# A 32-byte tile at the head of a pool of a Trainium2 kernel (GLA, HGRN2, mLSTM and a convolutional FFN, one step)

## The chip, the cores and the metric

The kernel runs on one core of one Trainium2 chip. The metric is the device time of one execution in microseconds. The program is one launch; its five engines are TensorE (PE; its weight loads are listed as PEld), VectorE (DVE), ScalarE (ACT), GpSimd (POOL) and SyncE (SP, which only issues transfers here).

## The reference

One inference step of a one-layer encoder over 1024 prompt frames and 32 frames of a running stream, all float32. A mixer of three kinds of recurrent heads is followed by a feed-forward part with a causal convolution; the change touches the last matrix product.

```python
def conv_ffn(xn, buf, w_up, conv_w, conv_b, w_down):
    up = xn @ w_up                                      # (T, 1024) @ (1024, 5632)
    up, buf = causal_dwconv(up, buf, conv_w, conv_b)
    gate, val = jnp.split(up, 2, axis=-1)
    return (jax.nn.gelu(gate, approximate=True) * val) @ w_down, buf    # (T, 2816) @ (2816, 1024)
...
h, st_new = mixer(rms_norm(x, g_mix_pre[l]), st, lb_all[l], w_in[l], ...)
x = x + rms_norm(h, g_mix_post[l])
h, ffn_buf = conv_ffn(rms_norm(x, g_ffn_pre[l]), ...)
x = x + rms_norm(h, g_ffn_post[l])
```

## The kernel before

The program runs in this order: input projection and mixers (interleaved), output projection (`zp`, with the weight `woh`/`wol` as moving operand and the transposed rows `ch`/`cl` as stationary one), up projection (accumulators `pux`, `puw`, `puy`, `puz`), down projection (accumulators `q`, `x`), final norm.

Every large product is made of three matmuls. A float32 operand is split into a rounded half and the rest (`split`, lines 105 to 110: ScalarE copies the rounded half, line 107, and VectorE subtracts for the rest, line 110). `mm3` (lines 100 to 103) then adds half x half (L101), half x rest (L102) and rest x half (L103) into one accumulator; its first operand is stationary, its second moving. In the profile such a matmul reads `out<-moving,stationary`.

The up and the down projection use a seven-product (Strassen) form. For the down projection, `down_all` runs seven kinds of product in the order P2, P1, P4, P6, P5, P7, P3. Each kind has 11 blocks (`NP`), one per pair of feature tiles. A block has two operands of 512 columns: `h` from rows of the activated hidden layer (`hts`, loaded by `load_h`) and `w` from the weight (`wraws`, loaded by `down_raw`, or its sums prepared in DRAM, `ws_d`). `down_operands` splits both. `run` then makes, for each of four 128-column slices of `h` as stationary operand, an `mm3` with all 512 columns of `w` moving into one of four accumulator banks: 12 matmuls of 128x512 a block, 132 a kind, 924 in all. During P2 and P1, `sample_products` (line 1462) adds four narrower float32 matmuls a pair of blocks for the 32 stream frames, straight from `ht` and the raw weight. During P4 and P6 VectorE also makes the sums of hidden rows that later kinds need (lines 1497 to 1506). After each of the four row slices of P3, VectorE, ScalarE and GpSimd norm the rows and SyncE stores them (lines 1635 to 1637).

The kernel is written in a framework that orders each engine's instructions by its own model of time, and that places tiles in SBUF pool by pool, each tile on a multiple of 32 bytes in its partition. The places follow from the code, and the built program lists them. The pool `ph` is opened by `freed` (line 1754), which runs in the last block of the up projection, when the pool `px` of the up projection's operands has been closed. It holds the hidden rows `ht11` to `ht21`, four raw weight buffers, four `h` operands (tag `hop`), and one early `w` operand, that of P2's first block, which `ahead` splits with `early=True`. All other `w` operands lie in the pool `p4` (`praw[1]`, tag `op`), two raw weight buffers in `p4r`. A row of 1060 float32 is 4240 bytes and takes up 4256 in the pool; all other tiles of `ph` have 4096.

Byte addresses in the partition, as built, before the change:

| operand | tiles | first address | modulo 64 | modulo 512 |
|---|---|---|---|---|
| `h` of the down projection (stationary) | 4 in `ph`, 4096 apart | 83,680 | 32 | 224 |
| `w` of the down projection (moving) | 7 in `p4`, 4096 apart | 25,856 | 0 | 256 |
| `w` of P2's first block | in `ph` | 95,968 | 32 | 224 |
| raw weights in `ph` | 4 | 63,040 | 0 | 64 |
| `ht11`, `ht12`, ... | in `ph` | 54,528 | 0 and 32 | varies |
| `woh`, `wol` of `zp` (moving) | in `p2` | 147,360; 180,128 | 32 | 416 |
| `ch`, `cl` of `zp` (stationary) | in `p2`, 2048 apart | 216,992; 223,136 | 32 | 416 |
| up projection, stationary | in `p4` | 25,856 | 0 | 256 |
| up projection, moving, 272 columns | in `px` | 54,528 | 0 | in steps of 64 |
| up projection, moving, 256 columns | in `px1` | 156,640 | 32 | 480 |

The rest of a split operand lies 2048 bytes behind its rounded half, and a slice of 128 columns 512 bytes behind the one before it.

Of the kernel before, what the change touches and what calls it, by code (L numbers as in the profile page):

```python
# [8 lines left out]
F32 = mybir.dt.float32  # L9
# [82 lines left out]
def body(ctx: ExitStack, tc: tile.TileContext, a: dict):  # L92
# [1236 lines left out]
    def up_finish(py, f, uu):  # L1329
# [15 lines left out]
        sp.dma_start(h_d[f], ys[0])  # L1345

    def up_all(pw_, W0, X, uus, py, freed, ahead, begun):

        raw, W, summed = {}, {0: W0}, []
        late = None  # L1350
        for f in range(NF):
            uu = uus[f % len(uus)]
            if f + 1 < NF:
                raw[f + 1] = up_raw(f + 1)
            for s in range(2):
                if s == 1 and f + 1 < NF:
                    ops = up_operands(f + 1, raw.pop(f + 1))
                    W[f + 1] = next(ops)
                    for _ in ops:
                        pass  # L1360
                if f or s:
                    blk = up_block(pw_, f, s, W[f], X[s], uu)
                    next(blk)
                    next(late, None)
                    if f == NF - 1 and s == 1:
                        freed()
                    m = (2 * f + s - 3) * len(SUMS) // 34
                    while len(summed) < min(m, len(SUMS)):
                        sum_weights(*SUMS[len(summed)])
                        summed.append(m)  # L1370
                    if s == 0:
                        up_finish(py(), f - 1, uus[(f - 1) % len(uus)])
                        W.pop(f - 1)
                    next(blk)
                else:
                    blk = begun
                yield
                next(blk)
                late = blk
                yield  # L1380
# [4 lines left out]
    praw, ph, EARLY = [], [], 3  # L1385
# [24 lines left out]
    def down_raw(kind, p):  # L1410

        key = (kind, p if kind in ("P1", "P2") else p // 2)
        if key in wraws:
            return
        own = len(wraws) % 6 < 2
        r = (praw[0] if own else ph[0]).tile([128, 2, 512], F32, tag="raw", name=f"wr{kind}_{p}", bufs=2 if own else 4)
        if kind in ("P1", "P2"):
            f = p + NP * (kind == "P2")
            behind["SP"] = sp.dma_start(r.rearrange("p j n -> p (j n)"), a["w_dn"][f])
        else:  # L1420
            n = min(2, NP - p)
            src = a["w_dn"][NP + p:NP + p + n, :, 512:].rearrange("f p n -> p f n") if kind == "P3" else \
                ws_d[{"P5": 0, "P7": 1, "P6": 2, "P4": 3}[kind]][:, p:p + n, :]
            behind["SP"] = sp.dma_start(r[:, :n, :], src)
        wraws[key] = r
# [3 lines left out]
    def load_h(pool_, f):  # L1429
        hts[f] = pool_.tile([128, NCOL], F32, name=f"ht{f}")  # L1430
        with tc.issue_after(behind["SP"].ins):
            sp.dma_start(hts[f], h_d[f])
# [321 lines left out]
    def freed():  # L1754
        pxs.close()
        ph.append(phs.enter_context(tc.tile_pool(name="ph", bufs=1, side="left")))
        for p in range(EARLY):
            down_raw("P2", p)
            load_h(ph[0], NP + p)
        down_raw("P2", EARLY)  # L1760
# [5 lines left out]
    for i, _ in enumerate(up_all(pw_, W0, X, uus, lambda: py[0], freed, ahead, blk)):  # L1766
        if i == 1:

            with tc.issue_after(done[0].ins), tc.issue_after(kept["c6"].ins):
                for x in last:  # L1770
                    next(x)
            X[1] = col_operands([px1] * 2, {f"B{k + 1}{j + 1}": x1[:, 4 * k:4 * k + 4, j, :] for k in range(2) for j in range(2)}, 1)
            p6s.close()
            p5s.close()
            py.append(p9s.enter_context(tc.tile_pool(name="p9", bufs=1, side="right")))
# [140 lines left out]
```

## Time and profile before

| | us |
|---|---|
| median of 3 runs | 1386.83 |
| lowest, highest | 1385.41, 1388.37 |
| the profiled execution | 1389.22 |
| its span, first to last instruction | 1387.5 |
| its mean granted TensorE clock | 0.983 of full speed |

The down projection's matmuls start at 1143.8 us of the span and the last one starts at 1377.1 us; what follows is the norm and the store of the last rows. In the profile's list of instructions in order of time each row has a start, a duration, the engine, the line, the operation with `out<-in`, the shapes and a count. Neighbouring rows of equal kind are merged, with the count behind `x`. The duration of a matmul contains a modelled end and overlaps with its successor, so the time that a matmul takes of the engine is the step from its start to the next one's. In the table of stages, a row has the stretch, its length, then each engine's busy time with its number of instructions, the granted TensorE clock (1.00 is full speed), and the DMA share and rate.

### The profile page before, as it was taken

The numbers are of one execution on the slowest core, as the hardware profiler recorded it, in microseconds if no ns is written. First come the engines' busy times: TensorE is split into PE (matmuls) and PEld (weight loads), VectorE is DVE, ScalarE is ACT, GpSimd is POOL, SyncE is SP. The second block draws the span as 40 slices with busy tenths as digits, with TensorE's granted clock in tenths as the row PEclk, the third lists the DMA queues.
The fourth block names the chain that finished last, engine by engine and source line by source line (L and its number), as shares of the span: only waits on it lengthen the run. The fifth ranks groups of instructions, "written<-read, shape, count | busy, mean of one in ns | idle before, by whom it ended". The sixth has DMA issues, their size and how long they took to land.

```text
span 1387.5 us, 29219 instructions
## 1 busy us (share of the span) xinstructions
PE 1341.0 (97%) x11472; PEld 1206.8 (87%) x11472; DVE 1029.7 (74%) x1916; ACT 706.6 (51%) x1369; POOL 316.0 (23%) x529
## 2 busy tenths in 40 slices
PE   6999999999999999999989999999999999999997
PEld 5999889898889887867889999999999996678885
DVE  4786568768587569685888888888888876498556
ACT  4555547446474446342665545545555544444552
POOL 5532411225112154222111112121121110010005
PEclk9999999999999998999999999999999999999999
DMA  8599869776789936443413475555365239645425
GB/s 342 199 326 350 276 228 307 235 263 228 249 263 322 310 96 211 152 142 90 165 52 135 142 176 146 142 142 160 108 169 135 89 133 392 245 155 152 129 99 122
DMA packets 125825, 269.72 MB, mean 194 GB/s; under 512 B 24007, under 2 KB 59367, under 8 KB 125607
## 3 DMA queue, kind: packets, MB, share of 16 engines
q1 hardware_dynamic: 111959, 245.43, 52.4%
q0 software_dynamic: 8928, 18.09, 7.0%
q10 hardware_dynamic: 4800, 4.33, 0.9%
q8 instruction: 90, 1.47, 0.4%
q14 instruction: 48, 0.39, 0.1%
HBM read 206.72 MB, written 86.18 MB: 211 GB/s over the span
## 4 chain that ended last, share of the span: by engine, by line
PE 76%; DVE 10%; ACT 5%; DMA 4%; issue 2%; POOL 1%; SPq 1%; DVEq 0%; POOLq 0%; ACTq 0%
PE pux L101 5%; PE pux L102 5%; PE pux L103 4%; PE pv L101 4%; PE pv L103 4%; PE pv L102 3%; PE puw L102 3%; PE puw L103 3%; PE puw L101 3%; PE q L101 3%; PE q L102 3%; PE q L103 3%; PE x L101 2%; PE x L102 2%; PE x L103 2%
## 5 line engine op out<-in xcount | busy, mean ns | idle before, releaser
L1341 DVE SCALAR_TENSOR_TENSOR y<-uu,fconv_sb,y 128x1060 f32<-128x1060 f32 x88 | 116.3, 1321 | 35.5 <-ACT y L1339 34.6
L1277 ACT COPY c<-pux 128x272 f32<-128x272 f32 (+1 forms) x132 | 49.4, 377 | 52.1 <-PE pux L103 48.5
L101 PE MATMUL pv<-wt_0h,xh 128*128 128x256 f32 (+2 forms) x195 | 57.9, 297 | 6.7 <-ACT xh L321 4.8
L1339 ACT ACTIVATE y<-uu,fconv_sb 128x1060 f32<-128x1060 f32 x44 | 56.3, 1279 | 11.8 <-POOL uu L1335 10.4
L101 PE MATMUL zp<-woh,ch 128*128 128x512 f32 (+1 forms) x144 | 60.0, 418 | 1.9 <-DVE z L1156 1.2
L1338 POOL COPY fhalo<-uu 128x2 f32<-128x2 f32 x44 | 16.6, 376 | 188.0 <-DVE uu L1282 188.0
L102 PE MATMUL zp<-wol,ch 128*128 128x512 f32 (+1 forms) x144 | 58.3, 405 | 0.0
L103 PE MATMUL zp<-woh,cl 128*128 128x512 f32 (+1 forms) x144 | 58.3, 406 | 0.0
L103 PE MATMUL pv<-wt_0h,xl 128*128 128x256 f32 (+2 forms) x195 | 56.9, 292 | 0.4 <-DVE xl L322 0.4
L102 PE MATMUL pv<-wt_0l,xh 128*128 128x256 f32 (+2 forms) x195 | 56.4, 289 | 0.1
L103 PE MATMUL pv<-wt_1h,xl 128*128 128x256 f32 (+2 forms) x195 | 56.5, 290 | 0.0
L102 PE MATMUL pv<-wt_1l,xh 128*128 128x256 f32 (+2 forms) x195 | 56.2, 288 | 0.0
L101 PE MATMUL pv<-wt_1h,xh 128*128 128x256 f32 (+2 forms) x195 | 56.1, 288 | 0.0
L1517 POOL TENSOR_TENSOR gss<-gss 128x1 f32<-128x1 f32 (+1 forms) x9 | 7.8, 868 | 191.0 <-ACT gjk L1510 191.0
L220 POOL TENSOR_SCALAR hrs<-hss 128x5 f32<-128x5 f32 (+3 forms) x27 | 9.9, 367 | 161.5 <-DVE hss L922 160.0
L431 POOL TENSOR_TENSOR vg<-vth,gh 128x256 f32<-128x256 f32 (+1 forms) x36 | 30.6, 851 | 63.6 <-DMA vm<-v_d 23.3
L101 PEld LDWEIGHTS pv<-wt_0h,xh 128*128 128x128 f32 (+1 forms) x195 | 37.1, 190 | 8.9 <-ACT xh L321 5.7
L851 DVE TENSOR_TENSOR Qz<-x,qe 128x128 f32<-128x128 f32 (+1 forms) x106 | 29.9, 300 | 12.3 <-PE sc L720 11.7
L815 DVE COPY_PREDICATED P<-masks_sb,sc 128x352 f32<-128x352 int32 (+1 forms) x44 | 29.8, 677 | 12.4 <-PE sc L720 12.2
L103 PEld LDWEIGHTS pv<-wt_0h,xl 128*128 128x128 f32 (+1 forms) x195 | 37.2, 191 | 1.2 <-DVE xl L322 0.9
L102 PEld LDWEIGHTS pv<-wt_0l,xh 128*128 128x128 f32 (+1 forms) x195 | 37.2, 191 | 0.6 <-POOL wt_0l L110 0.5
L101 PEld LDWEIGHTS pv<-wt_1h,xh 128*128 128x128 f32 (+1 forms) x195 | 37.1, 190 | 0.4 <-issue 0.2
(1718 smaller groups left out, 5409.4 us busy)
## 6 DMA issues: line engine op xcount, KB each, us to landing
wrP<-in_w_dn SPq DMA_DIRECT2D x27, 512.0 KB, 3.7
h_d<-y SPq DMA_DIRECT2D x22, 530.0 KB, 2.8
ht<-h_d SPq DMA_DIRECT2D x22, 530.0 KB, 8.8
wt_0r<-in_w_tok SPq DMA_DIRECT2D x21, 512.0 KB, 5.6
wt_1r<-in_w_tok SPq DMA_DIRECT2D x21, 512.0 KB, 6.7
ws_d<-in_w_dn POOLq DMA_DIRECT2D x20, 512.0 KB, 9.3
wrP<-ws_d SPq DMA_DIRECT2D x20, 512.0 KB, 4.0
wt_0l<-lt_d SPq DMA_DIRECT2D x14, 512.0 KB, 3.9
```

Source lines behind the costliest of these rows:

```text
L101: pe.matmul(ps, lh[0], rh[0], start=first, stop=False, **kw)
L102: pe.matmul(ps, lh[0], rh[1], start=False, stop=False, **kw)
L103: return pe.matmul(ps, lh[1], rh[0], start=False, stop=last, **kw)
L220: pool.tensor_scalar(out, ss, 1.0 / width, eps, op0=ALU.mult, op1=ALU.add)
L431: pool.tensor_tensor(o[:n], th[:n], gh[:n, c0:c0 + 256], op=ALU.mult)
L815: dve.copy_predicated(dst, mk.broadcast_to([n, 11, *mk.shape[2:]]), src)
L851: dve.tensor_tensor(Qp[:, 2 * i, :, :n // 2].rearrange("p e (m c) -> p e m c", c=c), second(x4[:, f:f + 1], c).broadcast_to([128, 2, n // ...
L1277: kept[name] = act.copy(t, ps)
L1338: behind["POOL"] = pool.tensor_copy(fhalo[:, j, :], u[:, NCOL - 2:NCOL])
L1339: act.activation(y, u, AF.Identity, scale=fconv[:, j, 2:3], bias=fconv[:, j, 3:4])
L1341: dve.scalar_tensor_tensor(y, uu[i][:, s:s + NCOL], fconv[:, j, s:s + 1], y, op0=ALU.mult, op1=ALU.add)
L1517: pool.tensor_tensor(ss[:n, 0:1], ss[:n, 2:3], ss[:n, 3:4], op=ALU.add)
```

## The change

`freed` allocates one more tile, of 8 float32 a partition, as the first one in `ph`. No instruction reads or writes it.

```diff
     def freed():
         pxs.close()
         ph.append(phs.enter_context(tc.tile_pool(name="ph", bufs=1, side="left")))
+        ph[0].tile([128, 8], F32, name="pad")
         for p in range(EARLY):
             down_raw("P2", p)
             load_h(ph[0], NP + p)
```

All 123 tiles that are placed in `ph` lie 32 bytes higher: `h` at 83,712 and so on (0 modulo 64, 256 modulo 512), the early `w` at 96,000 (0 and 256), the raw weights in `ph` at 63,072 (32 modulo 64); the rows `ht` swap, those at 0 modulo 64 going to 32 and those at 32 to 0. No other tile moves. The instructions of each engine, their order and their waits are the same as before.

## The prediction

> **What bounds the kernel now.** I read the page first, then the stages of the down projection, then the times at which single matmuls start.
>
> ```profile
> PE 1341.0 (97%) x11472; PEld 1206.8 (87%) x11472; DVE 1029.7 (74%) x1916; ACT 706.6 (51%) x1369; POOL 316.0 (23%) x529
> PE 76%; DVE 10%; ACT 5%; DMA 4%; issue 2%; POOL 1%; SPq 1%; DVEq 0%; POOLq 0%; ACTq 0%
> ```
>
> TensorE works through 97% of the span and carries 76% of the chain that ended last. The change touches only the down projection, the last 240 us. Its stages, with the busy time of each engine:
>
> ```profile
> core 0: us, PE busy (x) PEld busy (x) DVE busy (x) ACT busy (x) POOL busy (x), PEclk, DMA share, GB/s
> 1143.00:1183.00 40.00, 40.00 (x197) 28.25 (x197) 22.82 (x34) 18.32 (x31) 0.56 (x3) 1.00 1.01 395
> 1183.00:1223.00 40.00, 38.20 (x177) 24.11 (x175) 22.06 (x35) 17.98 (x33) 0.00 (x0) 1.00 0.63 234
> 1223.00:1253.00 30.00, 30.00 (x130) 23.96 (x129) 28.98 (x49) 14.23 (x31) 4.82 (x3) 1.00 0.40 121
> 1253.00:1285.00 32.00, 32.00 (x139) 25.71 (x138) 27.67 (x46) 16.64 (x31) 1.64 (x2) 1.00 0.48 144
> 1316.00:1346.00 30.00, 30.00 (x130) 24.12 (x129) 15.71 (x26) 13.68 (x26) 0.00 (x0) 1.00 0.38 132
> ```
>
> PE has no idle time but 1.8 us where P2 hands over to P1, and its granted clock is 1.00. So the stage ends when TensorE has streamed its matmuls, and what counts is the step from one start to the next. Here are the first starts of P7 and its last one:
>
> ```profile
> 1315.72 0.39 PE L101 MATMUL x<-P7w,P7h 128*128 128x512 f32 x1
> 1315.95 0.40 PE L102 MATMUL x<-P7w,P7h 128*128 128x512 f32 x1
> 1316.19 0.39 PE L103 MATMUL x<-P7w,P7h 128*128 128x512 f32 x1
> ...
> 1346.29 0.40 PE L103 MATMUL x<-P7w,P7h 128*128 128x512 f32 x1
> ```
>
> P7 has 11 blocks of 12 matmuls, 132; from its first to its last start are 131 steps, 30.57 us, **233.4 ns** a step. (The 0.39 us beside each is a modelled end; neighbours overlap.)
>
> The kernel has another phase of the same shape, three-term products of 512 moving columns on a 128x128 stationary: the output projection, `zp`. Its last unit, then unit 6:
>
> ```profile
> 672.21 0.39 PE L102 MATMUL zp<-wol,ch 128*128 128x512 f32 x1
> ...
> 681.05 0.39 PE L102 MATMUL zp<-wol,ch 128*128 128x512 f32 x1
> 658.64 0.39 PE L103 MATMUL zp<-woh,cl 128*128 128x512 f32 x1
> ...
> 660.90 0.39 PE L101 MATMUL zp<-woh,ch 128*128 128x512 f32 x1
> 671.00:681.00 10.00, 10.00 (x45) 8.26 (x45) 9.01 (x10) 8.48 (x21) 1.14 (x3) 1.00 0.59 211
> ```
>
> 39 steps in 8.84 us are **226.7 ns**, at the same clock 1.00, though VectorE and ScalarE are busier around it (9.01 and 8.48 of 10 us) than around P7 (15.71 and 13.68 of 30). Unit 6 changes the accumulator bank after every third matmul, as the down projection does, and still takes 2.26 us for 10 steps. So neither the clock, nor other engines, nor the change of banks makes the 6.7 ns between the two phases. What is left is where the operands lie. In `zp` the moving operand (`woh`, `wol`) and the stationary one (`ch`, `cl`) have the same remainder, 416, modulo 512 bytes, and every slice that a matmul takes keeps it. In the down projection the moving `w` has remainder 256 and the stationary `h` 224: 32 bytes apart.
>
> **The change part by part.** No instruction is added, removed or moved, and no wait; 123 tiles of `ph` lie 32 bytes higher. Four things can follow.
>
> *Products.* `h` gets remainder 256 modulo 512, as `w` has: the two operands are then placed to each other as in `zp`. Of the 924 products the first block of P2 already had equal remainders (its `w` is allocated in `ph` too and moves along), so 912 change. At zp's step that is 912 x (233.4 - 226.7) ns = 6.1 us. Whether this comes from the equal remainders is not shown by two phases alone, and the one block inside P2 with equal remainders reads:
>
> ```profile
> 1144.47 0.39 PE L102 MATMUL q<-P2w,P2h 128*128 128x512 f32 x1
> 1144.69 0.39 PE L103 MATMUL q<-P2w,P2h 128*128 128x512 f32 x1
> 1144.92 0.40 PE L102 MATMUL q<-P2w,P2h 128*128 128x512 f32 x1
> ...
> 1146.79 0.39 PE L101 MATMUL q<-P2w,P2h 128*128 128x512 f32 x1
> ```
>
> 10 steps in 2.32 us, 232 ns, with one step of 0.22 that P7 doesn't show: neither phase's rhythm. But zp also needs some matmuls after a break to find its own:
>
> ```profile
> 616.59 0.40 PE L102 MATMUL zp<-wol,ch 128*128 128x512 f32 x1
> ...
> 618.45 0.39 PE L101 MATMUL zp<-woh,ch 128*128 128x512 f32 x1
> ```
>
> These first 8 steps after a transpose take 1.86 us, 232 ns, like the block of P2. The bounds of the price are therefore 233.4 ns (no gain) and 226.7 ns (6.1 us); I take the second, less what breaks cost.
>
> *Breaks.* The sample rows' matmuls interrupt the products:
>
> ```profile
> L1462 PE MATMUL s<-wrP,ht x88: 592/605/618, 1153.0 to 1222.7; 128*32 128x512 f32 x88
> 1191.08 1.07 PE L1462 MATMUL s<-wrP,ht 128*32 128x512 f32 x8
> ```
>
> Eight a group make 11 groups; with the start of P2 and two pauses at the handover to P1, 14 breaks. Each loses up to 8 x (232.5 - 226.7) = 46 ns of the gain: 0.6 us. The sample matmuls' own operands move as well (`ht`, and four of six weight buffers from a multiple of 64 to 32 past one). Nothing shows their price; scaled by the same 6.7/233.4 to either side, the 88, some 1.07 us a group, could move by 11 x 1.07 x 2.9% = 0.3 us. I take 0 and keep both ends.
>
> *VectorE, ScalarE and transfers.* The split of `h` writes, and that of `w` reads, at shifted addresses:
>
> ```profile
> L110 DVE TENSOR_TENSOR P2h<-ht,P2h x11: 685/690/693, 1142.6 to 1175.9; 128x512 fp32r<-128x512 f32 x11
> L110 DVE TENSOR_TENSOR P2w<-wrP,P2w x11: 684/689/694, 1136.0 to 1170.0; 128x512 fp32r<-128x512 f32 x11
> ```
>
> One writes 32 past a multiple of 64, the other on one, and both take 684 to 694 ns: price 0. VectorE could still eat the gain where it is nearly full, 28.98 of 30 us in P4. The tightest operand there, `h` of block 4, is ready at 1235.22 and first needed at 1236.39:
>
> ```profile
> 1234.55 0.67 DVE L110 TENSOR_TENSOR P4h<-ht,P4h 128x512 fp32r<-128x512 f32 x1
> 1236.39 1.10 PE L103 MATMUL q<-P4w,P4h 128*128 128x512 f32 x4
> ```
>
> VectorE's burst begins with sums that wait for the end of P1, so it starts earlier by what P2 and P1 save; the 4 blocks of P4 before this use save 48 x 6.7 = 0.3 us, under the 1.17 us of slack. That cover holds. In P2, whose first 40 us run at DMA share 1.01, a faster TensorE asks for its loads sooner; if loads set its pace, its 132 products lose at most 0.9 us, which I put into the range.
>
> *The end.* The last 48 matmuls finish the four row blocks one after another, each followed by a chain on VectorE:
>
> ```profile
> 1369.12 0.69 DVE L1635 TENSOR_TENSOR ca<-ca,q 128x512 f32<-128x512 f32 x1 [1.45 <-PE q L103]
> 1379.32 0.69 DVE L1635 TENSOR_TENSOR ca<-ca,q 128x512 f32<-128x512 f32 x1
> ```
>
> The first waits for PE, the last no longer does (no idle before it). What PE saves in the 36 matmuls between is hidden: 36 x 6.7 = 0.2 us off the gain.
>
> **Sum:** 6.1 - 0.6 - 0.2 = 5.3 us. The profiled execution took 1389.22 us with a span of 1387.5; it would take 1383.9. The median of the runs shown is 2.4 us below it, 1386.83, so the forecast is 1386.8 - 5.3 = 1381.5 us.
>
> **The rivals.** *Nothing happens* (1386.8 us): the rhythm of `zp` has another cause, such as both operands standing 32 past a multiple of 64 and not their equal remainders; `h` and `w` come to stand on such multiples. For it: the block of P2 with equal remainders didn't fall into the rhythm. Against it: that block had 12 matmuls in an unusual order, and zp's 232 ns after a break look the same. [...]
>
> *Slower.* Both operands on multiples of 64 is what the 272-column products of the up projection have, beside the 256-column ones whose moving operand is 32 past one:
>
> ```profile
> 901.05 0.29 PE L102 MATMUL pux<-B11l,A_10h 128*128 128x272 f32 x1
> ...
> 908.11 0.28 PE L101 MATMUL puy<-B21h,A_10h 128*128 128x256 f32 x1
> 1143.06 0.28 PE L101 MATMUL puw<-B22h,S_21h 128*128 128x256 f32 x1
> ...
> 1143.76 0.86 PE L101 MATMUL q<-P2w,P2h 128*128 128x512 f32 x3
> ```
>
> 56 steps in 7.06 us are 126.1 ns, 0.464 ns a column; the 256-column ones take 0.70 us for 6, 0.456 a column. If aligned reads really run at 0.464, 512 columns take 237.4 ns, 4.0 more than now: 924 x 4.0 = 3.7 us, 1390.5 us. Its place is every product; it decides from a step of 236.5 ns on (3.0 ns x 924 = 2.8 us). Against it: a fixed part in each step could just as well make the difference, and `zp`'s operands, 32 past a multiple of 64 both, run at 0.443.
>
> **How the numbers follow.** The forecast gets 0.78, nothing 0.12, slower 0.10. Runs of this kernel spread by 0.2%, 2.8 us, and smaller differences aren't told from none; so the same numbers are the chances of faster, same and slower. The likeliest case's own range is 1379.7 (all 6.1 us, 0.3 from the sample matmuls, 0.7 for the medians' scatter) to 1383.6 (P2 paced by its loads, 0.3 lost on sample matmuls, scatter). For 8 in 10 the range must take in no change: up to 1387.4.
>
> **What would show it.** Right: P7's 131 steps take 29.7 us, and all stages from P1 to P3 shrink by some 0.9 us each, while everything before P2 keeps its times. Wrong in the main step: P7 still takes 30.6 us (no change) or over 31.0 (slower). Wrong in the cover: P7 shrinks, but PE shows new idle time in P2 before operands that loads bring, or in P4 before VectorE's.

## The result, and the profile after

| | before | changed |
|---|---|---|
| median, us | 1387.22 (18 runs, 1383.87 to 1390.29) | 1382.01 (18 runs, 1378.89 to 1385.98) |
| ratio, 95% interval | | 0.9969 (0.9960 to 0.9979) |
| span of the profiled execution, us | 1387.5 | 1382.8 |
| first to last start of the down projection, us | 233.3 | 229.7 |
| P7, 131 steps, us | 30.57 | 29.69 |

The ratio is the time of the changed kernel by that of the kernel before. By the medians the kernel became 5.2 us faster, where 5.3 were forecast; the interval allows 2.9 to 5.5. Two later measurements of it gave 0.9975 (0.9960 to 0.9990) and 0.9947 (0.9929 to 0.9965).

The list in order of time of the changed kernel, first and last start of P7, as the prediction showed them of the kernel before:

```profile
1312.62 0.39 PE L101 MATMUL x<-P7w,P7h 128*128 128x512 f32 x1
1312.85 0.39 PE L102 MATMUL x<-P7w,P7h 128*128 128x512 f32 x1
...
1342.31 0.39 PE L103 MATMUL x<-P7w,P7h 128*128 128x512 f32 x1
```

131 steps in 29.69 us are 226.6 ns, zp's rhythm. P4 went from 32.53 to 31.65 us, P6 from 34.30 to 33.32, P5 and P3 from 30.57 to 29.69 like P7 (first to last start of each kind). P2 went from 39.31 to 39.00 only, and P1 grew, from 40.94 to 41.92, because of the handover from P2 to P1. The table of stages and the list there:

```profile
1186.00:1192.00 6.00, 5.42 (x20) 3.46 (x20) 2.02 (x4) 1.82 (x5) 0.00 (x0) 0.72 0.88 352
1186.58 1.45 PE L101 MATMUL x<-P1w,P1h 128*128 128x512 f32 x4 [1.23 <-ACT P1w L107]
1187.83 0.63 PE L102 MATMUL x<-P1w,P1h 128*128 128x512 f32 x1
1188.26 0.63 PE L103 MATMUL x<-P1w,P1h 128*128 128x512 f32 x1
...
1190.39 0.56 PE L102 MATMUL x<-P1w,P1h 128*128 128x512 f32 x1
```

After two pauses the granted clock stands at half for 3.4 us (0.72 over these 6 us), and matmuls start 427 ns apart. That costs some 1.8 us here; the kernel before had no half clock in the down projection. Without it the stage would have shrunk by 5.5 us in place of 3.6, going by the kernels below that have the short step and no half clock (227.7 to 228.0 us). The span shrank by 4.7 us, but 1.2 of them stand ahead of the down projection, which starts at 1142.5 us in place of 1143.8; the three profiles of the changed kernel have this start between 1142.5 and 1143.8, so that part is scatter.

### The profile page after: what moved, and what is told of

It is laid out like the page before. It is cut to its first block, busy times and chain, and to the rows that moved or that the text cites. A ratio compares the mean times of both kernels' runs of the same rounds, so it can differ in the third digit from the quotient of the medians.

```text
span 1382.8 us, 29219 instructions
## 1 busy us (share of the span) xinstructions
PE 1335.3 (97%) x11472; PEld 1205.1 (87%) x11472; DVE 1029.2 (74%) x1916; ACT 704.8 (51%) x1369; POOL 316.9 (23%) x529
## 4 chain that ended last, share of the span: by engine, by line
PE 72%; DVE 12%; ACT 6%; DMA 6%; issue 2%; POOL 1%; SPq 1%; DVEq 0%; ACTq 0%; POOLq 0%
PE pux L101 5%; PE pux L102 5%; PE pux L103 4%; PE puw L102 3%; PE puw L103 3%; PE puw L101 3%; PE q L101 3%; PE q L102 3%; PE q L103 3%; PE pv L103 3%; PE pv L101 3%; PE pv L102 2%; PE zp L101 2%; PE x L101 2%; PE zp L103 2%
## 5 line engine op out<-in xcount | busy, mean ns | idle before, releaser
L103 PEld LDWEIGHTS pv<-wt_1h,xl 128*128 128x128 f32 (+1 forms) x195 | 36.8, 189 | 0.6 <-issue 0.2
```

The lines of the kernel that those rows point to most:

```text
L103: return pe.matmul(ps, lh[1], rh[0], start=False, stop=last, **kw)
```

## The experiments

The theory at this point: the step of a matmul depends on the distance between its stationary and its moving operand in the partition, and equal remainders make it short at 512 columns. Its chief rival is that both operands must stand on multiples of 64. Distances below are stationary minus moving address.

**Both on multiples of 64, but 64 apart.** The change with another size of the tile:

```diff
-        ph[0].tile([128, 8], F32, name="pad")
+        ph[0].tile([128, 24], F32, name="pad")
```

> The new tile has 96 bytes in place of 32: both operands of the down projection still begin at a multiple of 64, but h is now 64 bytes past w's remainder modulo 512. Theory A (what counts is that both stand on multiples of 64): P7's 131 steps stay at 226.7 ns, 29.7 us, and the time is some 5 us under the kernel before. Theory B (what counts is that both have equal remainders modulo 512, or modulo 128 or 256): the step goes back above 230 ns, P7 to 30.2 us or more, and at least half of the gain is gone. Theory C (only the remainder modulo 64 of one to the other counts): as A.

The ratio is 0.9991 (0.9975 to 1.0007). P7 in its list in order of time:

```profile
1312.32 0.40 PE L101 MATMUL x<-P7w,P7h 128*128 128x512 f32 x1
...
1342.89 0.39 PE L103 MATMUL x<-P7w,P7h 128*128 128x512 f32 x1
```

30.57 us again, 233.4 ns a step: theory A falls, and with it C, since here the distance is a multiple of 64. Standing on multiples of 64 is worth nothing by itself.

**Equal, but 32 past a multiple of 64.** To the changed kernel:

```diff
     p4 = p4s.enter_context(tc.tile_pool(name="p4", bufs=1, side="left"))
+    p4.tile([128, 120], F32, name="pad4")
```

> The changed kernel with 480 more bytes ahead of the w operands: w and h both have remainder 224 modulo 512, that is, both 32 past a multiple of 64, and equal. Theory A (multiples of 64): the down projection's step goes back to 233 ns, P7 to 30.6 us. Theories B and C (equal remainders): it stays at 226.7 ns, P7 29.7 us. The stationary operands of the up projection and the moving ones of its 272-column products move along by the same 480 bytes; the 256-column ones change from a distance of 224 to one of 256 modulo 512, for which nothing shows a price, so the whole time is not the test here.

```profile
1318.24 0.39 PE L101 MATMUL x<-P7w,P7h 128*128 128x512 f32 x1
...
1347.94 0.39 PE L103 MATMUL x<-P7w,P7h 128*128 128x512 f32 x1
```

29.70 us, 226.7 ns a step, with `h` at the remainder 224 that it has in the kernel before, where the step is 233.4. Where the operands stand doesn't count; that they stand alike does. The whole time is 0.9984 (0.9965 to 1.0004) of the one before: the up projection's 256-column matmuls, now 256 bytes apart, take 119.6 ns (118.2 in the changed kernel and the one before; mean step between neighbouring matmuls of this width, longer breaks left out), and its stage 483.2 us from first to last start (479.4 in the changed kernel). This profile also has the half clock at the handover.

**The same fault put into `zp`.** To the kernel before:

```diff
         gm = p2.tile([128, 1024], F32, name="gm")
+        p2.tile([128, 8], F32, name="pad2")
```

> The kernel before, with 32 bytes put between the moving and the stationary operands of the output projection, which have equal remainders before; the moving ones then stand on multiples of 64, the stationary ones 32 past. If the distance of the operands makes the step (A, B and C): zp's steady step goes from 226.7 to about 233 ns; over its 384 matmuls of full height, whose mean with the restarts was 228.6 ns, that is 384 x 4.8 ns = 1.8 us more. If the fast step of zp has another cause: 226.7 ns as before and no difference in time. The down projection stays at 233.4 ns in both.

One of its ten executions, the profiled one, took 2539 us, with matmuls 445 ns apart in the down projection; why is not known. The other nine give 0.9992 (0.9975 to 1.0009). It was run again:

> The same edit as e_zp32, whose profile was taken in an execution of 2537 us and can't be read. As there: with 32 bytes between the operands' remainders zp's steady step goes from 226.7 to about 233 ns, some 1.8 us in all, if the distance makes the step; it stays at 226.7 if zp's rhythm has another cause. The down projection stays at 233.4 ns.

Its list in order of time, in the last unit of `zp`:

```profile
671.15 0.39 PE L102 MATMUL zp<-wol,ch 128*128 128x512 f32 x1
...
681.18 0.39 PE L103 MATMUL zp<-woh,cl 128*128 128x512 f32 x1
```

43 steps in 10.03 us, 233.3 ns, where the kernel before had 226.7. So 32 bytes between the operands take the short step away, just as their removal brings it. The 1.8 us expected are too small to be told in the whole time: the ratios 0.9992 and 1.0004 (0.9987 to 1.0021) leave them undecided.

**Equal remainders in the up projection's 256-column matmuls.** To the changed kernel, behind the moving operands of those matmuls (`px1`):

```diff
             X[1] = col_operands([px1] * 2, ...)
+            px1.tile([128, 56], F32, name="padx")
```

> The changed kernel with 224 bytes behind the moving operands of the 256-column products of the up projection, so that they have remainder 256 modulo 512 as their stationary operands have (distance 224 before). [...] If the saving needs a long moving operand: 117 to 118 ns as before, and the time of the changed kernel. If it grows with the width: about 3 ns, 6 us.

The 224 in this text is counted from the stationary to the moving operand; as distances are counted here it is 32 modulo 256. The saving that it speaks of is the 6.7 ns of the 512-column step; half of that on 22 x 7 x 12 = 1848 matmuls is its 6 us. The same 36 matmuls in the list of the changed kernel, then of this one:

```profile
786.69 0.28 PE L101 MATMUL pux<-B11h,A_4h 128*128 128x256 f32 x1
...
790.83 0.28 PE L103 MATMUL puz<-T4h,A_4h 128*128 128x256 f32 x1
```

```profile
786.30 0.28 PE L101 MATMUL pux<-B11h,A_4h 128*128 128x256 f32 x1
...
790.50 0.28 PE L103 MATMUL puz<-T4h,A_4h 128*128 128x256 f32 x1
```

35 steps take 4.14 us, then 4.20. Both expectations fail: over the whole stage the step grows from 118.2 to 119.6 ns, the stage takes 482.1 us from first to last start in place of the changed kernel's 479.4, and the ratio to the kernel before is 0.9976 (0.9959 to 0.9993). What helps 512 columns hurts 256.

**A map.** In place of more cases, a kernel of bare matmuls: one moving and one stationary tile, both filled with zeros, and a loop like `run`'s, five times over for each width and distance. Only the stationary operand moves. The loop, with its constants written out:

```diff
+    for n in (512, 384, 288, 272, 256):
+        for d in range(16):
+            o = 8 * d
+            for rep in range(5):
+                for i in range(4):
+                    c = o + 128 * i
+                    mm3(banks[i][:, :n], (H[:, c:c + 128], H[:, 512 + c:640 + c]), (W[:, 0, :n], W[:, 1, :n]), rep == 0, rep == 4,
+                        skip_group_check=True)
```

> Leaves out the whole computation: zeros are stored as outputs, and TensorE runs 80 groups of 60 three-term matmuls from one moving tile and one stationary tile, for 512, 384, 288, 272 and 256 columns and, at each width, with the stationary operand 0, 32, 64, ... 480 bytes past the moving one's remainder modulo 512. What is read is the step between starts by group. Theory B1 (equal remainders modulo 512 alone are special): 226.7 ns at 512 columns for distance 0 and about 233 for all 15 others. B2 (equal modulo 128 or 256): 226.7 also at 128, 256 and 384, or at 256. At 256 columns the runs so far show 118 ns at 224 and 120 at 0 and 256, so another distance than 0 should be the best there; for a law of N + 32 cycles at distance 0: 226.7, 173.3, 133.3, 126.7 and 120.0 ns for the five widths.

The law named last is the line through two steps measured before, 226.7 ns at 512 columns and 120 at 256: 0.417 ns a column, with the time of 32 columns, 13.3 ns, on top. The first start of each group of 60 in its list in order of time, at 512 columns from distance 256 on, and at 256 columns from 0 on; a group's time divided by 60 is its step. The rows of 512 columns end with the first group of 384, those of 256 with distance 256:

```profile
117.15 0.39 PE L121 MATMUL acca<-mov,sta 128*128 128x512 f32 x1
130.76 0.39 PE L121 MATMUL acca<-mov,sta 128*128 128x512 f32 x1
144.75 0.40 PE L121 MATMUL acca<-mov,sta 128*128 128x512 f32 x1
158.75 0.39 PE L121 MATMUL acca<-mov,sta 128*128 128x512 f32 x1
172.79 0.39 PE L121 MATMUL acca<-mov,sta 128*128 128x512 f32 x1
186.74 0.39 PE L121 MATMUL acca<-mov,sta 128*128 128x512 f32 x1
200.74 0.40 PE L121 MATMUL acca<-mov,sta 128*128 128x512 f32 x1
214.48 0.40 PE L121 MATMUL acca<-mov,sta 128*128 128x512 f32 x1
228.48 0.33 PE L121 MATMUL acca<-mov,sta 128*128 128x384 f32 x1
...
644.17 0.28 PE L121 MATMUL acca<-mov,sta 128*128 128x256 f32 x1
651.36 0.28 PE L121 MATMUL acca<-mov,sta 128*128 128x256 f32 x1
658.46 0.28 PE L121 MATMUL acca<-mov,sta 128*128 128x256 f32 x1
665.53 0.28 PE L121 MATMUL acca<-mov,sta 128*128 128x256 f32 x1
672.57 0.28 PE L121 MATMUL acca<-mov,sta 128*128 128x256 f32 x1
```

The first gap, distance 256, is 13.61 us; the next three are 13.99, 14.00 and 14.04, and among the last four only distance 448 (200.74 to 214.48) comes near with 13.74. At 256 columns distance 0 is the longest of those shown, 7.19 us, and 96 the shortest, 7.04. The mean of the last 39 steps of each group, in ns, by the distance modulo 256:

| columns | 0 | 32 | 64 | 96 | 128 | 160 | 192 | 224 |
|---|---|---|---|---|---|---|---|---|
| 512 | 226.7 | 233.4 | 233.4 | 234.2 | 232.2 | 233.3 | 228.9 | 233.3 |
| 384 | 173.3 | 173.3 | 174.6 | 173.3 | 176.1 | 176.7 | 173.3 | 176.6 |
| 288 | 131.6 | 133.3 | 133.2 | 133.3 | 133.4 | 131.6 | 132.2 | 133.3 |
| 272 | 125.4 | 126.7 | 123.4 | 123.3 | 126.7 | 126.6 | 126.6 | 125.6 |
| 256 | 120.0 | 118.4 | 117.8 | 117.3 | 118.6 | 119.9 | 117.8 | 117.8 |

The second half of the 16 distances repeats the first within 0.3 ns, but for 272 columns at 32 (126.7) and 288 (125.4). So the period is 256 bytes: B1 falls, B2 holds for 256 and not for 128. The kernels, which work on other numbers than zeros, fit in: 233.4 ns before (distance 224), 226.6 after (0), 233.4 at 64. From 100 to 750 us of this kernel ScalarE and GpSimd are busy for 0.00 us, VectorE has no instruction, and the DMA share is 0.00. So neither another compute engine nor a transfer makes the difference; what does, no run shows.

**The period in the kernel itself.** A tile of 288 bytes (`[128, 72]`), distance 256:

> The new tile has 288 bytes: h lies 256 bytes past w's remainder modulo 512. By the map (period 256): P7 at 226.7 ns a step, 29.7 us, and the time of the changed kernel, 0.996 to 0.998 of the one before. If only equal remainders modulo 512 counted: 233 ns and no gain.

```profile
1307.96 0.39 PE L101 MATMUL x<-P7w,P7h 128*128 128x512 f32 x1
...
1337.65 0.39 PE L103 MATMUL x<-P7w,P7h 128*128 128x512 f32 x1
```

29.69 us; the ratio is 0.9943 (0.9925 to 0.9961).

**A better distance elsewhere.** By the map, 96 is best for the 256-column matmuls of the up projection (they stand at 32). In the input projection the distance is 128; by the map 192 is better where the weight is stationary, and 64 where the rows are. First `padx` of 64 bytes, `[128, 16]`, in the changed kernel; then, on top of it, 64 bytes between the rows and the weights of the input projection:

```diff
-        return (p1.tile([128, 8, T], F32R, tag="xh", name=f"xh{g}"),
-                p1.tile([128, 8, T], F32R, tag="xl", name=f"xl{g}"))
+        t = (p1.tile([128, 8, T], F32R, tag="xh", name=f"xh{g}"),
+             p1.tile([128, 8, T], F32R, tag="xl", name=f"xl{g}"))
+        if g == 0:
+            p1.tile([128, 16], F32, name="pad1")
+        return t
```

> The changed kernel with 64 bytes behind the moving operands of the up projection's 256-column products, so that the stationary operand lies 96 bytes past the moving one modulo 256 (32 before). The map gives 118.4 ns at 32 and 117.3 at 96: 1848 x 1.1 = 2.0 us under the changed kernel if TensorE sets the pace there; no difference if VectorE does.

> As v_up96, and 64 bytes between the rows and the weights of the input projection: their distance goes from 128 to 192 where the weight is stationary (384 columns: 176.1 to 173.3 ns in the map; 288: 133.4 to 132.2) and from 128 to 64 where the rows are (256 columns: 118.6 to 117.8). 576 x 2.8 + 537 x 1.2 + 954 x 0.8 = 3.0 us less than v_up96 by the map, if TensorE sets the pace in the input projection; less where it waits for operands there.

> The same kernel as v_up96, on the chip of e_pad288, whose placement leaves the up projection as in the changed kernel. If the distance of 96 in the up projection is worth what its steps show (479.1 against 479.5 us for that stage in the two profiles), it is 0.0 to 0.1% under e_pad288; if the 0.3% between v_up96 and the changed kernel is real, 0.3%; the rest of that was then chance, among it the half clock at the handover, 1.7 us in the changed kernel's profiles and none in that of v_up96.

| | ratio to before | 256-column step, up | up stage | down stage |
|---|---|---|---|---|
| changed (first, second, third) | 0.9969, 0.9975, 0.9947 | 118.2 ns | 479.4, 479.5, 479.2 us | 229.7, 229.7, 229.3 us |
| distance 96 in the up projection (first, again) | 0.9943, 0.9954 | 117.7 ns | 479.1, 478.3 us | 227.7, 227.8 us |
| and the input projection | 0.9944 | 117.7 ns | 478.4 us | 227.9 us |
| `ph` 288 bytes on (up as changed) | 0.9943 | | 478.8 us | 228.0 us |

Half of the 1.1 ns appeared, and the stage's time lies within or just below the scatter of 480.1 to 478.8 us between kernels with the same up projection, the one before among them. The kernel with 288 bytes, which leaves the up projection alone, is as fast as the one with 96 beside it on one chip (0.9943 against 0.9954), so no gain of that edit is shown. A version that beats the changed kernel was not found. In the input projection the steps did shrink, from 118.7 to 114.3 ns at 256 columns and from 175.9 to 173.4 at 384. The 114.3 is below every value of the map at this width, so the map doesn't foretell these matmuls, and why is open. The stage didn't end sooner for it. Its stretch in the tables of stages, without and with the last edit:

```profile
10.00:507.00 497.00, 482.27 (x5189) 445.29 (x5190) 352.06 (x769) 268.30 (x556) 151.43 (x188) 0.99 0.81 272
```

```profile
10.00:509.00 499.00, 479.43 (x5193) 440.85 (x5194) 353.44 (x769) 268.32 (x556) 151.09 (x188) 0.98 0.80 271
```

TensorE works less, 479.4 of 499 us in place of 482.3 of 497, and has some 20 us without work in the stage, where the other eleven profiles have 14 to 17. The stage's last matmul starts at 509.2 us, among the 507.4 to 513.9 us of those eleven. So the shorter steps went into waiting. What sets the end there was not taken apart; with a scatter of 6 us, one profile couldn't show a small gain either.

**The half clock.** Two more profiles of the changed kernel were taken, one beside the kernels above:

> The changed kernel as it is, on the chip of the two kernels below. Every theory: 0.9955 to 0.998 of the kernel before, P7 at 226.7 ns a step. Its profile after the first showed the clock at half for 3.4 us at the handover from P2 to P1; if that is chance, this one need not show it, and the matmul stages from P2 to P3 shrink by the full 5 us.

> The changed kernel a third time. Both profiles of it show the granted clock at half for 3.4 us at the handover from P2 to P1 (1187 us), that of the same placement shifted by 256 bytes does not, and the stage costs 1.8 us more with it. If the drop belongs to the changed kernel: it is there again, at 1187 us. If it is chance (where the pause falls in the 3.4 us raster of the clock's changes): it may be missing, and the down projection then takes 227.9 us from first to last start in place of 229.7.

The drop is there in all three profiles of the changed kernel and in that of the kernel with both operands at 32. It is in none of the others with the short step: the 224-byte and both 64-byte `padx` runs, the input projection's, and `ph` at 288. That it stayed in both further profiles speaks for a cause in the changed kernel, but the kernels without it run the same matmuls at the handover. The drops of one execution lie multiples of 3.41 us apart (in the first profile of the changed kernel the next one starts 187.73 us after that of the handover, 55 times 3.413), and this raster can be reckoned on to the handover, whose two pauses (0.6 and 1.2 us, the same in all profiles) fall differently into its stretches. The stretch with the second pause in the first profile of the changed kernel, then in the first with distance 96, as tables of stages show them:

```profile
1183.93:1187.34 3.41, 1.72 (x6) 1.16 (x7) 1.94 (x4) 2.06 (x4) 0.00 (x0) 1.00 1.02 411
```

```profile
1179.74:1183.15 3.41, 1.94 (x7) 1.33 (x8) 1.95 (x4) 1.84 (x4) 0.00 (x0) 1.00 1.02 412
```

TensorE is idle for 1.7 us of the first stretch, and the clock drops at its end; it is idle for 1.5 us of the second, and the clock stays. So it is in all twelve profiles that the kernels here left of this place: the four with the drop have 1.61 to 1.81 us of idle time in one stretch, the eight without it 1.49 at most, the kernel before among them. At the handover the idle time within one stretch of the raster tells the two apart, but the bound isn't the same everywhere: near 700 us stretches with 1.25 and 1.28 us are followed by a drop in two profiles, and one with 1.30 us isn't in a third. The two pauses stretch over 2.8 us; by an estimate from these figures, a raster that lies at random against them has some 1.6 us of idle time in one stretch in about a third of the executions. The drop is in 4 profiles of 12; whether the three of three in the changed kernel are chance stays open.

## Why the prediction was right

*Products.* The main term held to the digit: 233.4 - 226.7 = 6.7 ns a matmul was forecast and P7 gave 6.7. The cause that it named, equal placement of both operands, was shown by taking it away in the down projection (64 apart), keeping it elsewhere (both at 32), and undoing it in `zp`. One detail was too narrow: the remainder that counts is that modulo 256, not 512. P2's first block, which made this doubtful, was finding its rhythm: its steps of 231, 236, 228, 233 and 231 ns come again in the changed kernel, where 226 and 227 follow them. In the kernel before 235, 231 and 236 follow; matmuls of the second block, whose operands are 32 bytes apart there, are already mixed in, since the rows up to the next break have five of line 102 and a block has four.

*Breaks.* Forecast were 0.6 us lost. In the profiles without the half clock P2 and P1 shrank by 0.4 to 0.7 and 0.6 us (to 38.6 to 38.9 from 39.3, and to 40.3 from 40.9), where 132 x 6.7 ns would be 0.9 each. So the two lost 0.5 to 0.8 us. Most of it is the breaks: the steps under 242 ns of both kinds have a mean of 228.0 to 229.0 ns in place of 226.7, some 0.4 us over both. The rest is in P2, where some of the profiles have up to four longer steps, of 242 to 336 ns, in the first blocks; loads may be the cause, but the second run of the `zp` experiment, whose P2 is no faster, has two of them as well. The sample matmuls, whose price was put at 0, take 11.93 us in all in the kernel before and 11.92 in the changed one; they stand in 12 groups, of eight or four, and not in 11.

*Cover.* VectorE kept up: P4, nearly full on that engine, shrank by the full 0.88 us. At the end the stretch after the last matmul's start grew from 10.4 to 10.5 us, 0.1 in place of the 0.2 forecast to be hidden. (The upper end of the likeliest case, 1383.6 us, adds up to 1383.4 from the terms that it names.)

*What the sum left out.* The half clock at the handover, 1.8 us of the changed kernel's profile. With it P1 grew by 1.0 us there, where all kinds from P2 to P3 were to shrink by 0.9, and the profile shows a gain of 3.5 us from the down projection on, not 5.3. How many of the other executions had the half clock is not known, nor whether the kernel before never has it. The median came out at the forecast all the same; its own distance from the kernel before varied from 3.0 to 6.8 us between the three measurements, so the agreement to 0.1 us is luck. The step and the 5.5 us of the stage without the half clock are what is firm.

*The rivals.* Nothing happens: refuted by P7's 29.69 us in place of 30.57. The cause that this rival names doesn't make the step: with equal remainders it is 226.6 ns with both operands on multiples of 64 and 226.7 with both 32 past one. Slower, because operands on multiples of 64 stream slowly: its premise fell with both kernels that stand there, 233.4 at 64 apart and 226.6 at 0. Its other premise, 0.464 against 0.456 ns a column, came from few steps: over the whole up projection the 272-column matmuls step by 126.0 ns and the 256-column ones by 118.2, 0.463 and 0.462 ns a column.

## What to carry to other kernels

Where two phases of one kernel have the same matmul and different steps at full clock, compare where their operands lie: on this chip these three-term matmuls with 512 moving columns take 226.7 ns when stationary and moving operand have the same address modulo 256, and 228.9 to 234.2 at the other multiples of 32, mostly 233. The best distance depends on the width (in the map 0 at 512 columns, 226.7 ns, and 96 at 256, 117.3 ns), so it is measured, not copied, and a pad is worth placing only where TensorE sets the stage's end: in the input projection a step of 114.3 ns in place of 118.7 left the last matmul's start at 509.2 us, among the 507.4 to 513.9 of the others. A change described by one property (multiples of 64) can work by another one that it happens to bring.

## What the runs showed that was not expected

The distance has a period of 256 bytes, and at distance 0 the steps of the 512-, 384- and 256-column matmuls (226.7, 173.3 and 120.0 ns) lie on a line, 0.417 ns a column plus 13.3 ns. Distance 0 has the shortest step at 512, shares it with three other distances at 384, and has the longest at 256. After a break the short step needs several matmuls to settle (in P2's first block of the changed kernel five steps of 228 to 236 ns come ahead of the first of 226 and 227). After two pauses of 1.8 us in all the clock stood at half for 3.4 us in 4 of 12 profiles; those four have 1.61 us or more of idle time in one stretch of a 3.41 us raster there, the other eight 1.49 us at most.
